# A diffusion layer on one core: the neighbourhood values' column blocks kept by row, and copied later

## The chip, the core and the metric

The kernel runs on one core of a Trainium2 chip. TensorE (PE) multiplies matrices, and its weight loads (PEld) run beside its products; VectorE (DVE), ScalarE (ACT) and GpSimd (POOL) work on elements; SyncE (SP) issues nearly all transfers, and 16 DMA engines carry them out. Each engine takes its own list of instructions in order and waits at semaphores for the others. The metric is the time of one execution in microseconds (us) on the device. All numbers are of one core.

## The reference, cut to what matters

One layer works on 1024 latent tokens (a grid of 16 rows by 64 columns) and 256 context tokens, 1024 wide. Half of the width goes through a gated DeltaNet (four heads of 128, scanned forward and backward in chunks), half through a neighbourhood attention (eight heads of 64). Then follow an output projection and a SwiGLU feed-forward.

```python
px = modulate(rms_norm(x, norm1_w[i]), sh1, sc1) @ w_in[i]
pc = modulate(rms_norm(ctx, norm1_w[i]), csh1, csc1) @ w_in[i]
...
dn_x, _, _ = gated_deltanet(px[..., :DN_IN], ..., s_ctx_f, s_ctx_b)
qx, kx, vx = na_qkv(px[..., DN_IN:], na_q_norm_w[i], na_k_norm_w[i])
qc, kc, vc = na_qkv(pc[..., DN_IN:], na_q_norm_w[i], na_k_norm_w[i])
na_x = neighborhood_attention(qx, kx, vx, kc, vc, na_rpb[i], rows)
x = x + g1 * (jnp.concatenate([dn_x, na_x], axis=-1) @ w_out[i])
x = x + g2 * swiglu(...)
```

In the neighbourhood attention a query sees 8 rows by 16 columns around it. The 64 columns are cut into four blocks of 16 queries, and all queries of a block read the same 32 columns of keys and values (`key_cols`); each query masks what lies outside of its window. The values that a column block needs are therefore 32 of each row's 64 columns, in all 16 rows: 512 tokens of 512 values.

## The kernel before, in words

The projections run from about 60 to 547 us, as a list of jobs. A job is one block of 128 output columns (or a wide one, whose result stays by token): `k`, `q`, `v` of the DeltaNet with their short convolutions, `nk`, `nq` of the attention, and `z`, the DeltaNet's output gate. The list ends with nq0 to nq2, q0, q1 (at the index `turn`), q2, q3, v0 to v3, nq3 and z0 to z3. For each job, in this order in the text:

- `prefetch` loads the weights of the job after it (L218, `wraw<-w_...` on SP). There is one raw buffer. ACT rounds it to a high part (L219, CAST `whi<-wraw`), POOL subtracts to get the low part (L221, `wlo<-wraw,whi`). There are two buffers of each part.
- PE makes the products in eight steps of 128 (L102, `blk<-hh,whi`, then `hl,whi`, then `hh,wlo`; hh and hl are the two parts of the tokens). `blk` with its number is the block's accumulator. A q, nq or z block takes 48 of these products (1024 tokens), a v block 72 (1280 tokens).
- After it ACT copies the block out (L506, `cr<-blk`; L483, `zt<-blk` for z). For q, k and v the five taps of the convolution follow on DVE (L515 and L520, `cacc<-cr,cw`), then an activation (L529, `cacc<-cacc`), and two jobs later the block's finish: its transposes on PE (L106, `m<-cst,cacc`) and what is stored from them.
- Beside the products, a step at a time, run background programs. `block_inverses` makes small inverses (N, L947 to L952). `preps` makes the twenty chunk systems of the DeltaNet: products `pr<-fx,kk` and `pr<-y,kk` on PE, with `kk` made on DVE (L1016) and copied on ACT (L1028), `y` copied on DVE (L1036), and stores `y_d` and `at_d` (L1052). `copies` issues the copies that this change is about.

The values of the attention, `nv_d`, are written by token in DRAM (L669). `vw_d` holds for each of the four column blocks (`cb`) its 32 columns of each row, by four groups of four rows (`ch`). The attention loads a column block of two heads at a time from it (L331, `vw<-vw_d`): 128 partitions by four groups of 128 values. Its loads of the first heads (L279 to L337: kT, qs, kh, kl, vc, bt, vw, v, y, kt) are issued at the end of the projections, once the chunk systems' buffers are free.

What is issued when isn't the order of the text: a scheduler sets each engine's list at build, by its own costs, within what the data allow. `tc.keep_in_program_order` holds the instructions that are given to it in the order in which they were written.

Of the kernel before, what the change touches and what calls it, by code (L numbers as in the profile page):

```python
# [9 lines left out]
F32 = mybir.dt.float32  # L10
# [18 lines left out]
BLKS = [0, 8, 24, 32]  # L29
# [62 lines left out]
def hybrid(ctx, tc, a, dbg):  # L92
    nc = tc.nc
    act, dve, pool, sp = nc.scalar, nc.vector, nc.gpsimd, nc.sync
# [16 lines left out]
    def pools(stack, name, side=None, bufs=1, **kw):  # L111
        if side:
            kw["side"] = side
        return stack.enter_context(tc.tile_pool(name=name, bufs=bufs, reuse_waits="tile", **kw))
# [6 lines left out]
    dram = ctx.enter_context(tc.tile_pool(name="dram", bufs=1, space=DRAM))  # L121
# [43 lines left out]
    nv_d = dram.tile([T, 512], F32, name="nv_d", tag="nv_d")  # L165
    nq_d = dram.tile([NAH, 2, ND, L], F16, name="nq_d", tag="nq_d")
    nk_d = dram.tile([2, NAH, ND, T], F16, name="nk_d", tag="nk_d")
    vw_d = dram.tile([128, 4, 4, 512], F32, name="vw_d", tag="vw_d")
    y_d = dram.tile([2, NCH, 128, 4, 128], F32, name="y_d", tag="y_d")
    at_d = dram.tile([2, 8, 128, 4, 128], F32, name="at_d", tag="at_d")  # L170
    x_d = dram.tile([128, 2, 2, NU, 32], F32, name="x_d", tag="x_d")
# [97 lines left out]
    def load(d, c, own=None):  # L269

        def tile(n):
            if own:
                return own.tile([128, 4, 128], F32, name=n, tag=f"{n}{d}")
            return (scan_v if n == "v" else scan_in).tile([128, 4, 128], F32, name=n, tag=n, bufs=3)

        old = chunks.pop(c, None)
        kT, qT, kt, v = old or (tile("kT"), tile("qT") if c >= 2 else None, tile("kt"), tile("v"))
        if not old:
            sp.dma_start(kT, kT_d[:, :, c * 128:(c + 1) * 128])  # L279
            sp.dma_start(fl(v), v_d[c * 128:(c + 1) * 128])  # L280
        y = tile("y")
        sp.dma_start(y, y_d[d, c])
        if not old:
            sp.dma_start(fl(kt), k_d[c * 128:(c + 1) * 128])
        at = None
        if c >= 2:
            if not old:
                sp.dma_start(qT, qT_d[:, :, (c - 2) * 128:(c - 1) * 128])
            at = tile("at")
            sp.dma_start(at, at_d[d, c - 2])  # L290
        if not old and c in TWICE:
            chunks[c] = kT, qT, kt, v
        ready[d, c] = kT, qT, kt, v, y, at, bool(old) or c not in TWICE
# [5 lines left out]
    def attention(nw):  # L299
# [18 lines left out]
        def biases(hp, half, cb):  # L318

            key = hp, half, CASE[cb]  # L320
            if tables[0] != key:
                out = lasting_bt[tables[1] % 2]
                for u, w0 in enumerate(WIN):
                    sp.dma_start(out[u][:, w0:w0 + 384], a["rpb"][2 * hp + u, half, CASE[cb]])
                tables[:] = key, tables[1] + 1
            return lasting_bt[(tables[1] - 1) % 2]

        def values(hp, half, cb):
            if (hp, cb) not in blocks:
                vw = nw.tile([128, 4, 128], F32, name="vw", tag="vw", bufs=3)  # L330
                sp.dma_start(vw, vw_d[:, cb, :, hp * 128:hp * 128 + 128])  # L331
                blocks[hp, cb] = vw
            return blocks[hp, cb][:, half:half + 3]

# [59 lines left out]
        heads = {0: [load(0), load(1)]}  # L394
        vcs = {0: context(0)}
        bt, vw = biases(*order[0]), values(*order[0])
        yield 1
        old = None
        for n, (hp, half, cb) in enumerate(order):
            at = n % len(TILES)  # L400
            if at in (4, 6) and hp + 1 < NAH // 2:
                heads.setdefault(hp + 1, []).append(load(2 * hp + at // 2))
                if at == 4:
                    vcs[hp + 1] = context(hp + 1)
            cur = pair(heads[hp], bt, vw, vcs[hp], half, cb, na[hp])
            next(cur)
            if old:
                next(old)
            if n + 1 < len(order):
                bt, vw = biases(*order[n + 1]), values(*order[n + 1])  # L410
            yield 1
            if old:
                next(old)
            old = cur
            yield 1
# [5 lines left out]
    with ExitStack() as bs:  # L421
# [3 lines left out]
        hp = pools(bs, "hp", "right")  # L425
# [653 lines left out]
        inv = len(jobs)  # L1079
        jobs += [Block("nk", i) for i in range(3)] + [Wide(0, zp), Block("nk", 3)]  # L1080
        jobs += [Block("nq", i) for i in range(3)] + [Block("q", 0)]
        turn = len(jobs)
        jobs += [Block("q", i) for i in (1, 2, 3)]
        later = len(jobs)
        values = inv + 3
        queries = range(turn - 1, later)
        jobs += [Block("v", i) for i in range(4)] + [Block("nq", 3)]
        gates = len(jobs)
# [2 lines left out]
        def windows():  # L1091
            vlat = nv_d[CT:].rearrange("(r c) d -> r c d", c=64)
            for cb in range(4):
                for ch in range(4):
                    sp.dma_start(vw_d[:, cb, ch], vlat[4 * ch:4 * ch + 4, BLKS[cb]:BLKS[cb] + 32])
                    yield

        copies = Background()

        def blk(n):  # L1100
            return jobs[n] if 0 <= n < len(jobs) and isinstance(jobs[n], Block) else None
# [9 lines left out]
        for n in range(2, len(jobs) + 2):  # L1111
            j = jobs[n] if n < len(jobs) else None
            if n == inv:
                bg2.drain()
                bg2s.close()
                early.close()
                psum.append(bs.enter_context(tc.tile_pool(name="psa", bufs=1, space=PSUM)))
                bg.add(block_inverses())
                bg.add(preps())
            if n == gates + 1:  # L1120
                bg.drain()
                late.close()
                cps.close()
                zo.append(pools(bs, "zo", "right", 2))
                fw = pools(attn, "nw", "left", 2)
                fill = attention(fw)
                next(fill)
                sl0 = pools(begins, "sl0", "left")
                KN, KB = (fw.tile([128, 2, NCH, 4], F32, name=n, tag=n, bufs=1) for n in ("KN", "KB"))
                dve.tensor_tensor(KN, KD, NB, OP.mult)  # L1130
                dve.tensor_tensor(KB, KD, B, OP.mult)
                for d in range(2):
                    load(d, ORDER[d][0], sl0)
            if n + 1 < len(jobs):
                jobs[n + 1].prefetch()
            fin = blk(n - 2) if n - 2 not in done else None
            fin = fin.finish() if fin else iter(())
            nrm = blk(n - 1)
            taps = nrm and nrm.later or iter(())
            if isinstance(j, Wide):  # L1140
                for t, _ in enumerate(j.tiles()):
                    next(fin, 0)
                    for _ in range(3):
                        next(taps, 0)
                    if t == 4 and nrm:
                        nrm.norm()
                        for _ in fin:
                            pass
                        fin = nrm.finish()
                        done.add(n - 1)  # L1150
                        nrm = None
                    bg2.step(2)
                    if n < turn:
                        bg.step(2)
                    if n >= turn:
                        bg.step(5)
            elif j:
                for k in range(KT):
                    j.mm([k])
                    next(taps, 0)  # L1160
                    next(taps, 0)
                    if k >= 3:
                        next(fin, 0)
                    bg.step(1 if n < turn else 3)
                    bg2.step(1)
                    copies.step(2)
                j.evac()
            for _ in fin:
                pass
            done.add(n - 2)  # L1170
            if isinstance(j, Wide) and n == values:
                copies.add(windows())
            if nrm:
                nrm.norm()
            if isinstance(j, Block) and j.later is None:
                j.silu()
# [213 lines left out]
    class Stream:  # L1390
# [67 lines left out]
        def next(self, n=2):  # L1458

            while len(self.got) < n:  # L1460
                self.make()
            out = [self.got.pop(0) for _ in range(n)]
            return out
# [400 lines left out]
```

## Time and profile before

| | |
|---|---|
| time, median of 3 runs | 1508.61 us (1508.04 to 1511.2) |
| the profiled execution | 1507.78 us |
| its span | 1506.0 us |
| mean granted clock of TensorE | 0.994 |
| DMA traffic | 267.35 MB, 178 GB/s over the span |
| the copies into `vw_d` | 16, issued from 220.3 to 260.6 us |
| the loads from `vw_d` | 16, issued from 531.1 to 726.0 us |

The profile is of one execution, and its times count from the span's start; 1.8 us of the execution lie outside of the span. Busy times are of each engine, and idle time matters on an engine only if others wait for it. In the lists of instructions, a row gives the start, the duration, the engine, the line and the operation with its output and inputs, and in brackets how long the engine sat idle before it and what ended that.

### The profile page before, as it was taken

The page shows a single profiled execution, that of the slowest core. Times are in us where ns is not written, and L with a number is a line of the kernel's source. Part 1 is how long each engine was busy: PE and PEld are TensorE (multiplying, and loading weights), DVE is VectorE, ACT ScalarE, POOL GpSimd, SP SyncE. Part 2 cuts the span into 40 slices and gives each one's busy share as a digit, 9 for nine tenths or more (in the row PEclk, how much of TensorE's full clock was granted, in tenths as well). Part 3 has the DMA queues.
Part 4 walks back from the last instruction along what each step waited for, and adds up shares of the span by engine and source line. Part 5 has one row for each costly group of instructions (what it writes and reads, how often), then busy time and mean ns, then how long its engine had stood idle before and what let it go on. Part 6 is the DMA issues. An engine that isn't in the chain of part 4 may idle for free.

```text
span 1506.0 us, 23093 instructions
## 1 busy us (share of the span) xinstructions
PE 1449.8 (96%) x8365; PEld 1201.0 (80%) x8365; DVE 1004.4 (67%) x1892; ACT 696.2 (46%) x1321; POOL 193.4 (13%) x223
## 2 busy tenths in 40 slices
PE   5999998899999999999989999999999999999998
PEld 2789787678877778887877878888888888888887
DVE  4886579455598427679966499666655557698642
ACT  6443461584266526566742374333333334354440
POOL 0154500343124221211100000000000000000000
PEclk9999999999999999999999999999999999999999
DMA  9377133555377799986349106333333334898742
GB/s 368 117 234 239 57 92 121 191 168 190 118 243 238 220 284 265 262 228 193 110 134 332 72 30 203 113 105 105 102 102 105 106 105 161 287 349 286 240 145 84
DMA packets 198851, 267.35 MB, mean 178 GB/s; under 512 B 15232, under 2 KB 106960, under 8 KB 197712
## 3 DMA queue, kind: packets, MB, share of 16 engines
q1 hardware_dynamic: 198016, 265.49, 54.7%
q8 instruction: 66, 1.08, 0.3%
q14 instruction: 49, 0.40, 0.1%
q10 hardware_dynamic: 720, 0.37, 0.1%
HBM read 201.01 MB, written 68.98 MB: 179 GB/s over the span
## 4 chain that ended last, share of the span: by engine, by line
PE 51%; DVE 6%; ACT 3%; DMA 2%; issue 1%; SPq 0%; ACTq 0%; DVEq 0%
PE ps L102 45%; PE sc L102 5%; PE sc L106 2%; DMA wad<-wa 1%; ACT pt L377 1%; ACT ex L365 1%; DVE ex L363 1%; DVE acc L255 1%; DVE x L1618 1%; DVE x L1594 0%; DVE ex L367 0%; DVE ulo L1449 0%; DVE lT L1589 0%; DVE ws L1444 0%; ACT x L1598 0%
## 5 line engine op out<-in xcount | busy, mean ns | idle before, releaser
L102 PE MATMUL ps<-hT,uhi 128*128 128x512 f32 x496 | 146.8, 390 | 0.8 <-DVE e L1739 0.7
L102 PE MATMUL ps<-lT,uhi 128*128 128x512 f32 x496 | 146.4, 389 | 0.0
L102 PE MATMUL ps<-hT,ulo 128*128 128x512 f32 x496 | 146.3, 389 | 0.0
L102 PE MATMUL blk<-hh,whi 128*128 128x512 f32 (+1 forms) x456 | 138.0, 393 | 2.4 <-ACT hh L748 1.7
L102 PE MATMUL blk<-hh,wlo 128*128 128x512 f32 (+1 forms) x456 | 129.7, 377 | 0.0
L102 PE MATMUL ps<-hB,uhi 128*128 128x512 f32 x436 | 129.1, 390 | 0.0
L102 PE MATMUL blk<-hl,whi 128*128 128x512 f32 (+1 forms) x456 | 129.0, 376 | 0.0
L102 PE MATMUL ps<-lB,uhi 128*128 128x512 f32 x436 | 128.8, 389 | 0.0
L102 PE MATMUL ps<-hB,ulo 128*128 128x512 f32 x436 | 128.8, 389 | 0.0
L1448 ACT CAST uhi<-ws 128x512 fp32r<-128x512 f32 x91 | 54.7, 622 | 145.5 <-PE ps L102 78.2
L1448 ACT CAST uhi<-wq 128x512 fp32r<-128x512 f32 x101 | 60.4, 621 | 132.8 <-PE ps L102 69.4
L1449 DVE TENSOR_TENSOR ulo<-wq,uhi 128x512 fp32r<-128x512 f32 x101 | 67.1, 687 | 65.6 <-ACT uhi L1448 36.4
L102 PEld LDWEIGHTS ps<-hT,uhi 128*128 128x128 f32 x496 | 93.0, 188 | 20.7 <-ACT uhi L1448 1.1
L102 PEld LDWEIGHTS ps<-lT,uhi 128*128 128x128 f32 x496 | 93.0, 188 | 19.7 <-DVE lT L1602 0.5
L102 PEld LDWEIGHTS ps<-hT,ulo 128*128 128x128 f32 x496 | 93.1, 188 | 19.4
L102 PEld LDWEIGHTS ps<-hB,uhi 128*128 128x128 f32 x436 | 81.8, 188 | 17.5 <-issue 0.5
L102 PEld LDWEIGHTS ps<-lB,uhi 128*128 128x128 f32 x436 | 81.8, 188 | 17.3 <-DVE lB L1602 0.4
L102 PEld LDWEIGHTS ps<-hB,ulo 128*128 128x128 f32 x436 | 81.8, 188 | 17.0
L102 PEld LDWEIGHTS blk<-hh,wlo 128*128 128x128 f32 x456 | 80.1, 189 | 17.6 <-issue 1.7
L102 PEld LDWEIGHTS blk<-hl,whi 128*128 128x128 f32 x456 | 80.7, 189 | 15.5
L102 PEld LDWEIGHTS blk<-hh,whi 128*128 128x128 f32 x456 | 76.5, 189 | 19.8 <-ACT hh L748 3.7
L1449 DVE TENSOR_TENSOR ulo<-ws,uhi 128x512 fp32r<-128x512 f32 x91 | 60.6, 685 | 36.2 <-ACT uhi L1448 28.0
(341 smaller groups left out, 3026.0 us busy)
## 6 DMA issues: line engine op xcount, KB each, us to landing
wq<-w_fo SPq DMA_DIRECT2D x99, 256.0 KB
wq<-w_gu SPq DMA_DIRECT2D x88, 256.0 KB
wad<-wa SPq DMA_DIRECT2D x64, 256.0 KB
t_d<-g SPq DMA_DIRECT2D x22, 512.0 KB
fr<-t_d SPq DMA_DIRECT2D x44, 256.0 KB
bt<-rpb SPq DMA_DIRECT2D x48, 192.0 KB
f_d<-g SPq DMA_DIRECT2D x33, 256.0 KB
fr<-f_d SPq DMA_DIRECT2D x33, 256.0 KB
```

The costliest lines, as they stand in the source:

```text
L102: i = nc.tensor.matmul(*args, **kw)
L106: i = nc.tensor.transpose(*args, **kw)
L255: dve.scalar_tensor_tensor(acc2, x, sc, acc2, op0=OP.mult, op1=OP.add)
L363: dve.tensor_tensor_reduce(ex, sc, bt, 1.0, -3.0e38, OP.add, OP.max, m[:, 0:1])
L365: act.activation(ex, ex, AF.Exp, bias=m[:, 1:2], accum_out=m[:, 2:3])
L377: act.copy(pt, sc)
L1448: act.copy(hi, self.raw[key])
L1449: dve.tensor_tensor(lo, self.raw[key], hi.bitcast(F32), OP.subtract)
L1618: dve.tensor_tensor(B[at][:, k], B[x][:, k], B.get(y, B["B11"])[:, k], OP.subtract)
```

## The change

`vw_d` becomes one array of 512 tokens for each column block, by row of the grid and then column. One copy for each column block takes the place of four: 16 rows in runs of 32 tokens by 512 values, 64 KB, where before a copy had four rows and 32 tokens, each token spread to another partition index, in runs of 2 KB. The bytes are the same, 4 MB. The sixteen copies went out two at a time from the job behind the second wide one on (from 220.3 us); the four go out one in each of the jobs q2, q3, v0 and v1, in the fifth of the eight steps, held in that order. The load `vw<-vw_d` keeps its shape, 128 partitions by four runs of 512 B.

```diff
-    vw_d = dram.tile([128, 4, 4, 512], F32, name="vw_d", tag="vw_d")
+    vw_d = dram.tile([4, 512, 512], F32, name="vw_d", tag="vw_d")
...
-                sp.dma_start(vw, vw_d[:, cb, :, hp * 128:hp * 128 + 128])
+                sp.dma_start(vw, vw_d[cb].rearrange("(n p) d -> p n d", p=128)[:, :, hp * 128:hp * 128 + 128])
...
-        values = inv + 3
...
             for cb in range(4):
-                for ch in range(4):
-                    sp.dma_start(vw_d[:, cb, ch], vlat[4 * ch:4 * ch + 4, BLKS[cb]:BLKS[cb] + 32])
-                    yield
+                tc.keep_in_program_order(nc.sync.dma_start(
+                    vw_d[cb].rearrange("(r c) d -> r (c d)", c=32),
+                    vlat[:, BLKS[cb]:BLKS[cb] + 32].rearrange("r c d -> r (c d)")))
+                yield
...
-                    copies.step(2)
+                    if k == 4:
+                        copies.step(1)
...
-            if isinstance(j, Wide) and n == values:
+            if n == turn:
                 copies.add(windows())
```

On PE the lists are the same up to the middle of q3; from there to the end of the projections many rows stand elsewhere, on all engines. Two places matter below.

The first is PE where v2 ends and v3 begins. Before, in PE's list (blk_3438 to 3440 are v2's accumulators, blk_3774 and 3775 v3's; pr_3800 is a product of a prep):

```order
L102 MATMUL blk_3438<-hh7_423,wlo_3311 128x256
L102 MATMUL blk_3439<-hh7_423,wlo_3311 128x512
L102 MATMUL blk_3440<-hh7_423,wlo_3311 128x512
L102 MATMUL blk_3774<-hh0_136,whi_3433 128x256
L102 MATMUL blk_3774<-hl0_137,whi_3433 128x256
L102 MATMUL blk_3774<-hh0_136,wlo_3434 128x256
L102 MATMUL pr_3800<-fx1_2479,kk_3522 128x96 x4
L102 MATMUL blk_3775<-hh0_136,whi_3433 128x512
```

The same place on PE in the changed kernel (blk_3426 to 3428 are v2's, blk_3762 to 3764 v3's; cacc_3415 is v1's convolution and cacc_3751 that of v2):

```order
L102 MATMUL blk_3426<-hh7_423,wlo_3298 128x256
L102 MATMUL blk_3427<-hh7_423,wlo_3298 128x512
L102 MATMUL blk_3428<-hh7_423,wlo_3298 128x512
L106 MATMUL m_3894<-cst_71,cacc_3415 128x128 x4
L106 MATMUL m_3929<-cst_71,cacc_3415 128x128 x4
L106 MATMUL m_3958<-cst_71,cacc_3415 128x128 x2
L106 MATMUL m_4176<-cst_71,cacc_3751 128x128 x4
L106 MATMUL m_4203<-cst_71,cacc_3751 128x128 x4
L102 MATMUL blk_3762<-hh0_136,whi_3421 128x256
L102 MATMUL blk_3763<-hh0_136,whi_3421 128x512
```

The transposes of v2 (cacc_3751) moved from the nq3 job, where they stand before, to the front of v3, right behind v2's own last products. On ACT the cast of v3's weights has moved too. Before, in ACT's list (whi_3433 are v3's weights, blk_3315 begins v1's copy-out):

```order
L529 ACTIVATE cacc_3303<-cacc_3303 128x1280
L612 COPY kk_3385<-m_3386 128x512
L612 COPY kk_3385<-m_3402 128x512
L219 CAST whi_3433<-wraw_3432 128x1024
L506 COPY cr_3428<-blk_3315 128x256
```

In the changed kernel ACT's list has it (whi_3421) behind v2's copy-out and activation (cr_3752, cacc_3751):

```order
L529 ACTIVATE cacc_3415<-cacc_3415 128x1280
L506 COPY cr_3752<-blk_3426 128x256
L506 COPY cr_3752<-blk_3427 128x512
L506 COPY cr_3752<-blk_3428 128x512
L529 ACTIVATE cacc_3751<-cacc_3751 128x1280
L219 CAST whi_3421<-wraw_3420 128x1024
```

It moved by a whole block and more: from ahead of v1's copy-out to behind v2's copy-out and activation.

The second place is SP at the last two weight loads, those of z2 and z3. Before, in SP's list (the y_d and at_d rows are the preps' last stores, zT_d and nq_d stores of z and nq3):

```order
L591 DMA v_d<-vt 128x10x128
L1052 DMA at_d<-at 128x512 x3
L218 DMA wraw<-w_z 128x8x128
L484 DMA zT_d<-zt 128x1024
L1052 DMA y_d<-y_2474 128x512
L1052 DMA y_d<-y_2475 128x512
L1052 DMA y_d<-y_2476 128x512
L574 DMA nq_d<-hl_4621 64x1024 x4
L1052 DMA y_d<-y_2477 128x512
L218 DMA wraw<-w_z 128x8x128
L279 DMA kT<-kT_d 128x4x128
L305 DMA qs<-nq_d 128x1024
```

In the changed kernel SP issues them here; ahead of the first row shown stand the last y_d store and thirteen more loads of the attention, from kT on, with no weight load among them:

```order
L337 DMA vc<-nv_d 128x2x128
L324 DMA bt_4711<-rpb 128x384 x2
L331 DMA vw<-vw_d 128x4x128
L284 DMA kt<-k_d 128x512
L279 DMA kT<-kT_d 128x4x128
L280 DMA v<-v_d 128x512
L282 DMA y<-y_d 128x512
L284 DMA kt<-k_d 128x512
L218 DMA wraw<-w_z 128x8x128
L484 DMA zT_d<-zt 128x1024
L324 DMA bt_4713<-rpb 128x384 x2
L331 DMA vw<-vw_d 128x4x128 x2
```

Both weight loads moved behind the attention's first 22 loads, the one of z2 by more than twenty rows. On PE the last product of the last prep (pr on y and kk) stands in both kernels ahead of z2; in the changed one it is the very last row ahead of it, and z2's and z3's 96 products follow in one piece.

## The prediction

> **What bounds the kernel now.** I read the totals and the slices first, to see which engine sets the time:
>
> ```profile
> PE 1449.8 (96%) x8365; PEld 1201.0 (80%) x8365; DVE 1004.4 (67%) x1892; ACT 696.2 (46%) x1321; POOL 193.4 (13%) x223
> PE   5999998899999999999989999999999999999998
> DMA  9377133555377799986349106333333334898742
> ```
>
> TensorE (PE) is busy for 96% of the span, and a slice below 9 is rare. So 55 us of the span are all that any change can win, while every microsecond in which PE is made to wait is lost in full. Next I read the windows of the projection phase, which holds all that the change touches (columns: window, its length, then busy time and count of PE, PEld, DVE, ACT and POOL, the granted clock, the DMA engines' share, GB/s):
>
> ```profile
> 240.00:260.00 20.00, 16.99 (x81) 13.61 (x79) 19.35 (x19) 3.58 (x5) 2.66 (x1) 0.99 0.29 112
> 260.00:280.00 20.00, 17.59 (x83) 14.36 (x84) 9.89 (x18) 6.46 (x9) 5.19 (x7) 0.84 0.38 130
> 280.00:300.00 20.00, 13.10 (x54) 9.96 (x54) 9.96 (x6) 14.61 (x24) 5.69 (x9) 0.93 0.68 225
> 500.00:520.00 20.00, 20.00 (x157) 14.31 (x157) 9.60 (x22) 14.20 (x23) 4.53 (x7) 1.00 0.62 198
> 520.00:540.00 20.00, 20.00 (x90) 16.58 (x89) 0.17 (x2) 3.11 (x5) 3.43 (x2) 1.00 1.02 289
> ```
>
> PE stands still for 12.3 us between 240 and 300, just behind the sixteen copies, and not at all from 500 to 540. In the two late windows, where the new order puts its work, there is nothing to win. Two waits make up the early 12.3 us (engine, line and operation that waited, what it waited for, us in total, times, longest):
>
> ```profile
> PE pr L102 <- DVE kk L1016: 6.9, 1, 6.9
> PE m L106 <- DVE N L952: 5.4, 1, 5.4
> ```
>
> The second is a chain of VectorE (DVE) products of the block inverses, on which no transfer has a say; it stays. The first hangs on the copies. On SyncE's (SP's) queue, in ScalarE's (ACT's) cast of the weights that the load behind them brings, and on PE:
>
> ```profile
> 237.17 9.99 SPq L1095 DMA_DIRECT2D vw_d<-nv_d  x6
> 247.26 2.36 SPq L669 DMA_DIRECT2D nv_d<-zt  x1
> 249.66 11.61 SPq L1095 DMA_DIRECT2D vw_d<-nv_d  x5
> 261.36 2.26 SPq L218 DMA_DIRECT2D wraw<-w_nqk  x1
> ```
>
> ```profile
> 270.81 0.62 PE L102 MATMUL blk<-hh,wlo 128*128 128x512 f32 x2
> 273.49 1.05 ACT L219 CAST whi<-wraw 128x1024 fp32r<-128x1024 f32 x1 [20.93 <-DMA wraw<-w_nqk]
> ```
>
> From 237.17 to 261.26 eleven copies and one store go through, 24.1 us; per copy that is 2.19 us for 256 KB, 119 GB/s, with the DMA share at 0.29 to 0.38. The weight load behind them lands so late that its cast starts at 273.49. A reader sees here what the old form costs: the queue, not the engines, is full.
>
> **The gain.** Sixteen copies go, and with them the block at 237 to 261. The weights would then be there long before; the cast must still wait for the buffer that PE's block up to 271.4 (270.81 and 0.62) reads, so it can start some 2.0 us sooner. What follows it on ACT and DVE leads to the kk product for which PE waits 6.9 us. I take 2.3 us, the 2.0 and a little less crowding on the way; the ends are 0 (the chain turns out to hang on something else) and 6.9 (the whole wait).
>
> **The four copies.** Each moves 1 MB in 16 runs. Their price is not in the trace. By the 119 GB/s of the old ones it is 8.8 us each; by the 289 GB/s of window 520 to 540 it is 3.6 us. They stand on SP behind the weight loads of q2, q3, v0 and v1 and ahead of those that are needed a block later (the shortest block lasts 10.9 us, by the copy-outs of z1 and z2 at 525.05 and 535.99 that are quoted below). At either price the next load still lands in time, so I take 0; below 0 nothing speaks for them, and the upper end is rival 3. For the rate, the Trainium skill ("DMA: Bandwidth & Descriptors", section on why a DMA increments its semaphore by 16) says that a transfer is shared over the largest number of engines up to 16 that divides the slowest dimension on both sides: 4 engines for the old 4 rows against 128, 16 for the new 16 against 16. The DMA share of 0.29 to 0.38 under a full queue agrees with 4 of 16 and some other traffic; by that rule a new copy runs at the full rate, and the sum stays as it is.
>
> **The new order.** The four copies may not be moved against each other, and the scheduler that writes the order at build comes out elsewhere from q3 on. The instructions are the same but for twelve copies fewer; every engine runs its list in order, so a row that stands too early makes all behind it wait. Nothing in the trace shows these places, and each is put together from durations of before.
>
> *v3's start on PE* (the first place shown with the change). The transposes of v2's convolution (cst,cacc) now stand ahead of v3's first product, and v3's cast stands behind v2's activation L529 on ACT. Both need all of v2's convolution, whose input is the block that PE has just ended. That chain, from a v block of before, on ACT, DVE and POOL:
>
> ```profile
> 390.51 1.05 ACT L219 CAST whi<-wraw 128x1024 fp32r<-128x1024 f32 x1 [2.38 <-PE blk L102]
> 391.47 1.34 ACT L506 COPY cr<-blk 128x256 f32<-128x256 f32 x3
> 401.75 1.27 ACT L529 ACTIVATE cacc<-cacc 128x1280 f32<-128x1280 f32 x1 [8.94 <-DVE cacc L520]
> ```
>
> ```profile
> 391.87 2.33 DVE L515 TENSOR_SCALAR cacc<-cr,cw 128x256 f32<-128x256 f32 x1 [9.44 <-ACT cr L506]
> 394.23 1.00 DVE L520 SCALAR_TENSOR_TENSOR cacc<-cr,cw,cacc 128x254 f32<-128x254 f32 x2
> 395.15 0.75 DVE L515 TENSOR_SCALAR cacc<-cr,cw 128x1024 f32<-128x1024 f32 x1
> 395.82 4.57 DVE L520 SCALAR_TENSOR_TENSOR cacc<-cr,cw,cacc 128x255 f32<-128x255 f32 x5
> 400.43 1.28 DVE L520 SCALAR_TENSOR_TENSOR cacc<-cr,cw,cacc 128x1022 f32<-128x1022 f32 x1
> ```
>
> ```profile
> 391.64 2.40 POOL L221 TENSOR_TENSOR wlo<-wraw,whi 128x1024 fp32r<-128x1024 f32 x1 [15.12 <-ACT whi L219]
> ```
>
> From the copy-out of the block at 391.47 to the end of the activation at 403.02 it takes 11.55 us, and then 1.05 for the cast: 12.6 us in which PE has nothing. The low part wlo (2.40 on POOL) is read by the third product of each step, and hides behind the six before it. In the old order the same 11.55 us ran beside a whole block of PE work: that cover is what goes. I take 12.6. The ends: 8, should the chain start earlier than PE's end, and 16, with wlo in full and the other DVE rows that stand between the taps.
>
> *z2's weights on SP* (the second place shown). Before, the load of z2's weights left SP a block ahead; now SP issues it behind the last y_d store and 22 loads of the attention. The rows of SP and ACT before:
>
> ```profile
> 503.24 0.55 SPq L218 DMA_DIRECT2D wraw<-w_z  x1
> ...
> 519.80 0.33 SPq L1052 DMA_DIRECT2D y_d<-y  x1
> 520.22 0.59 SPq L218 DMA_DIRECT2D wraw<-w_z  x1
> 520.90 0.68 SPq L279 DMA_DIRECT2D kT<-kT_d  x1
> ...
> 535.53 0.43 SPq L284 DMA_DIRECT2D kt<-k_d  x1
> ```
>
> ```profile
> 511.19 1.03 ACT L219 CAST whi<-wraw 128x1024 fp32r<-128x1024 f32 x1
> 525.05 1.09 ACT L483 ACTIVATE zt<-blk 128x512 f32<-128x512 f32 x2 [7.99 <-PE blk L102]
> 526.02 1.05 ACT L219 CAST whi<-wraw 128x1024 fp32r<-128x1024 f32 x1
> 535.99 1.09 ACT L483 ACTIVATE zt<-blk 128x512 f32<-128x512 f32 x2 [8.92 <-PE blk L102]
> ```
>
> z2's cast ran at 511.19, 14 us before z1 left PE (its copy-out is at 525.05). In the new order the y_d store needs the last pr product, and that is PE's last row ahead of z2. So from PE's end of z1: a copy of y and the store, 1.0 us (0.33 for the store, the rest is an estimate from the small DVE rows); the 22 loads (kT first, kt last), 520.90 to 535.96, 15.1 us; the issue of the weights, 0.6; their way, 3 us as an estimate, since the window 520 to 540 shows the engines full (1.02, 289 GB/s, so 512 KB alone take 1.8 us); the cast 1.05. Sum 20.7 us, and PE has nothing else, since z2 and z3 stand there without any other row between them. The ends: 15, if the loads go out without a pause, and 26, if the weights queue behind all of the 5.8 MB that such a window moves (20 us). z3's weights follow a block behind and stay covered.
>
> *The clock.* Each long stall is followed by slow products, as both waits of before show:
>
> ```profile
> 262.40:266.30 3.90, 3.89 (x18) 3.20 (x18) 1.72 (x5) 0.00 (x0) 0.00 (x0) 0.50 0.54 181
> 299.00:303.00 4.00, 3.91 (x16) 3.07 (x17) 0.72 (x2) 3.60 (x11) 2.53 (x8) 0.50 0.90 309
> ```
>
> About 4 us at half the clock cost 2.0 us a stall; two stalls, 4.0 us. The Trainium skill ("TensorE: Matmul & The Clock Gate", Part 1) gives the same window of about 3.4 us of activity before the clock is full again; by it the term would be 3.4 us for two.
>
> *Six smaller places.* At v0's start three preps (pr products that feed each other through ACT and DVE) stand bare on PE where before they lay between products of a block; at v1, v2, nq3 and z1 a cast stands behind the copy-out of the block just ended; in nq3 and z0 ten prep products lie back to back. One such round, on PE, ACT, PE:
>
> ```profile
> 504.70 1.03 PE L102 MATMUL pr<-fx,kk 128*128 128x96 f32 x8
> 505.77 0.48 ACT L1028 COPY kk<-pr 128x384 f32<-128x384 f32 x1 [0.32 <-PE pr L102]
> 506.55 0.99 PE L102 MATMUL pr<-y,kk 128*32 128x96 f32 x16
> ```
>
> From one pr to the next 1.85 us, of which PE works 1.03. At 0.8 of waiting a round, five to six rounds at v0 give 4.5; a cast behind a copy-out (1.34 and 1.05) gives up to 2.4 at v1, v2 and nq3, of which I take 1.6, 2.5 and 1.5; z0 gets 2, and z1, where tables and copies stand ahead of the cast too, 4. Sum 16 us, from 5 (most hidden by the slack of one block) to 24.
>
> *Attention's start.* Its loads come no later than before beside the end of z3, some sooner: -1.5 (0 to -3).
>
> **Sum**, against the profiled execution (1507.8; the median of the runs, 1508.6, is 0.8 above it): -2.3 + 0 + 12.6 + 20.7 + 4.0 + 16 - 1.5 = +49.5, so 1557.3, and 1558 against the median.
>
> **Rivals.**
> 1. *One large stall does not come.* If v3's 12.6 or z2's 20.7 with its 2 of clock is covered after all (say the store and loads go out while z1 still runs), and the small places cost 8 rather than 16: -2.3 + 12.6 + 2 + 8 - 1.5 = +19, 1527, or with z2's alone +27, 1536. For it: estimates of single stalls add up places that share slack. Against it: PE runs in order and at neither place is there a row to fill the gap. 0.14.
> 2. *Faster.* The window at 240 to 300 is the one place where PE waits for these copies. If the whole 6.9 us go, and all that the new order does to PE is to shift work between waits of the same length, the end is 1508.6 - 6.9 = 1502. It decides if v3's cast and z2's load both come before PE ends v2 and z1. Against it: both windows 500 to 540 are at 20.00 busy, so there is no wait to be given back, and z2's load stands behind a store that needs z1's last rows. 0.04; 0.02 for a change within 0.2%, about what a measurement of this kernel can tell from none.
> 3. *The copies are slow.* If a run of 64 KB were left to a quarter of the engines or less, 8.8 us each and more, the weights of v0 to v3 would come late as well: three times some 8 us on top, 1580. Against it: sixteen equal rows and a share of 1.02 where loads are well cut. 0.06.
>
> **Chances.** My forecast, both stalls and most of the small ones, 0.74; rival 1 0.14, rival 2 0.04 and 0.02 for no change, rival 3 0.06. The predicted time is the sum, 1558. The forecast's own bounds (v3 8 to 16, z2 15 to 26, the small places 5 to 24) do not all fall one way; half of the added distances gives 1541 to 1573. The range takes in rival 1 with z2's stall alone and ends short of rival 3: 1528 to 1576. Slower by over 0.2%: 0.74 + 0.14 + 0.06 = 0.94.
>
> **What would show it.** PE's waits in the new profile should name ACT's cast (or the transposes' cacc of L529) before v3 with 10 us or more, and ACT's cast L219 with some 20 us before z2, behind SP rows of kT, qs, kh, kl, bt and w_z in one piece; the clock should read 0.5 in the 4 us behind each. The wait of 6.9 us on kk should be 4 to 5, and the copies 2 to 9 us each on SP with no weight load late for them. It would be wrong if PE shows 20.00 in the window of z2's start, or if the new waits stand before other blocks than v3 and z2.

## The result and the profile after

The changed kernel takes 1570.68 us in the median (1566.7 to 1571.57, four runs), the kernel before 1509.13 on the same occasions: 1.0401 times as long, with a 95% interval from 1.038 to 1.0422. That is 61.6 us more, where 1558 was forecast. The profiled execution took 1566.7 us, its span is 1564.9.

The totals and slices of the changed kernel:

```profile
PE 1461.5 (93%) x8365; PEld 1210.1 (77%) x8365; DVE 997.7 (64%) x1892; ACT 697.9 (45%) x1321; POOL 193.3 (12%) x223
PE   5999998998978839999998999999999999999999
PEclk9999999999989969999999999999999999999999
```

PE does the same 8365 products, and its dips have moved: there is an 8 and a 7 where q3 to v3 lie, and two 8s and a 3 from nq3 to the z blocks, with 6 as the granted clock under the 3. PE's busy time is 11.7 us longer although it does no more work; 10.3 of them are counted below as lower clock. Its waits between 310 us (where nq2 is copied out) and 607 (the end of z3), of the changed kernel:

```profile
PE blk L102 <- ACT whi L219: 30.9, 4, 23.8
PE m L106 <- ACT cacc L529: 8.5, 1, 8.5
PE pr L102 <- DVE y L1036: 5.6, 6, 2.5
PE pr L102 <- DVE kk L1016: 5.4, 3, 2.3
```

With three more of 0.6 and 0.7 us they sum to 52.4 us. In the kernel before, the same stretch (to 547) has 1.5 us in all:

```profile
PE pr L102 <- DVE y L1036: 1.2, 2, 0.8
PE pr L102 <- ACT kk L1028: 0.3, 1, 0.3
```

The copy-out of nq2 came 2.7 us sooner than before (310.06 against 312.73), that of z3 59.8 later (606.70 against 546.86), and after it 0.9 are won back. So 62.5 us were lost between the two: 50.9 of waits, 10.3 of half clock (summed over windows of 2 us, busy time of PE by what was missing of the clock), and 1.3 that I can't place.

*The largest*, z2. The changed kernel on SP, then ACT and PE:

```profile
558.88 0.32 SPq L1052 DMA_DIRECT2D y_d<-y  x1
559.25 0.57 SPq L279 DMA_DIRECT2D kT<-kT_d  x1
...
574.41 0.43 SPq L284 DMA_DIRECT2D kt<-k_d  x1
574.88 0.58 SPq L218 DMA_DIRECT2D wraw<-w_z  x1
```

```profile
580.88 1.05 ACT L219 CAST whi<-wraw 128x1024 fp32r<-128x1024 f32 x1 [22.55 <-DMA wraw<-w_z]
```

```profile
581.97 1.22 PE L102 MATMUL blk<-hh,whi 128*128 128x512 f32 x2 [23.76 <-ACT whi L219]
```

PE ends its last pr product at 558.2. The store, the 22 loads in 15.6 us, 6.0 us from the issue of the weights to their cast, and the cast follow one another, with PE idle for 23.76 us. While the weights were on their way (574.88 to 580.88) the DMA engines' share was 1.09, at 380 GB/s: they shared the engines with the attention's loads.

*The second*, v3, on ACT and PE:

```profile
441.33 1.35 ACT L506 COPY cr<-blk 128x256 f32<-128x256 f32 x3 [5.43 <-PE blk L102]
450.85 1.27 ACT L529 ACTIVATE cacc<-cacc 128x1280 f32<-128x1280 f32 x1 [8.17 <-DVE cacc L520]
452.03 1.03 ACT L219 CAST whi<-wraw 128x1024 fp32r<-128x1024 f32 x1
```

```profile
452.18 1.97 PE L106 MATMUL m<-cst,cacc 128*128 128x128 f32 x8 [8.47 <-ACT cacc L529]
453.79 1.41 PE L102 MATMUL blk<-hh,whi 128*128 128x256 f32 x3
```

Between v2's last product and v3's first lie 12.1 us, 9.2 of them idle (8.47, and 0.69 ahead of a transpose of v1). The rest is transposes, which PE did elsewhere before.

*The clock*, in windows behind the waits at v3, z1 and z2 (length, busy times, clock, DMA share, GB/s):

```profile
452.00:457.20 5.20, 5.03 (x18) 4.44 (x19) 3.71 (x8) 1.06 (x2) 3.76 (x6) 0.50 0.00 0
535.00:540.00 5.00, 5.00 (x22) 4.12 (x22) 0.42 (x1) 4.86 (x12) 4.22 (x13) 0.57 0.16 58
582.00:586.50 4.50, 4.12 (x9) 2.82 (x10) 0.00 (x0) 0.00 (x0) 2.37 (x1) 0.50 0.56 158
```

A fourth stretch lies at 381 to 386, behind v0's waits, with a granted clock of 0.53. Each costs 2.4 to 2.7 us.

*The copies.* Each of the four takes SP 0.53 to 0.58 us, and the early load of weights now leaves SP as soon as its buffer is free:

```profile
252.87 0.60 SPq L218 DMA_DIRECT2D wraw<-w_nqk  x1
...
359.82 0.54 SPq L1093 DMA_DIRECT2D vw_d<-nv_d  x1
```

Its cast starts at 271.05 instead of 273.49, and PE's wait on kk is 3.26 us instead of 6.90. No weight load after q1 waits for a copy.

### The profile page after: what moved, and what is told of

Its sections match the earlier page's. It is cut to its first block, busy times and chain, and to the rows that moved or that the text cites. A ratio compares the mean times of both kernels' runs of the same rounds, so it can differ in the third digit from the quotient of the medians.

```text
span 1564.9 us, 23094 instructions
## 1 busy us (share of the span) xinstructions
PE 1461.5 (93%) x8365; PEld 1210.1 (77%) x8365; DVE 997.7 (64%) x1892; ACT 697.9 (45%) x1321; POOL 193.3 (12%) x223
## 4 chain that ended last, share of the span: by engine, by line
PE 49%; DVE 6%; ACT 3%; DMA 2%; issue 1%; SPq 0%; ACTq 0%; DVEq 0%
PE ps L102 43%; PE sc L102 4%; PE sc L106 2%; DMA wad<-wa 1%; ACT pt L377 1%; ACT ex L365 1%; DVE ex L363 1%; DVE acc L255 1%; DVE x L1619 1%; DVE x L1595 0%; DVE ulo L1450 0%; DVE lT L1590 0%; DVE ex L367 0%; DMA wraw<-w_out 0%; DMA at<-at_d 0%
## 5 line engine op out<-in xcount | busy, mean ns | idle before, releaser
L221 POOL TENSOR_TENSOR wlo<-wraw,whi 128x1024 fp32r<-128x1024 f32 x21 | 53.8, 2560 | 274.4 <-ACT whi L219 255.1
```

What stands on the lines that cost most here:

```text
L221: lo_engine.tensor_tensor(o, r, h.bitcast(F32), OP.subtract)
```

## The experiments

Two theories stood against each other: that the loss is all of the new order, and that the four large copies themselves, so late, hold something up. Ratios are to the kernel before, in the same rounds. In some of these kernels the lines of the text lie two lower than in the changed kernel.

**Loads and casts held ahead.** From q1 on, `issue_after` puts all that is written later on SP and ACT behind the weight load and its cast:

```diff
+            casts.append(act.copy(h, r))
...
             if n + 1 < len(jobs):
                 jobs[n + 1].prefetch()
+            with ExitStack() as first_:
+                if n >= turn and n + 1 < len(jobs):
+                    first_.enter_context(tc.issue_after(casts[-1].ins))
+                    first_.enter_context(tc.issue_after(casts_sp[-1].ins))
```

> The changed kernel with its four copies as they are, but from q1 on each weight load and each cast is held ahead of what is written after it on SP and on ACT; in the order that comes of it no cast stands behind the copy-out of the block before, and both z loads stand ahead of the attention's loads. Theory of the order: all the loss goes, 1503 to 1508 us, 2 to 5 below the kernel before, since the 2.7 us won at 260 to 300 stay. Rival, that the four copies (their rate, or the traffic at their time) hold up the weight loads: the copies still run in the blocks q2 to v1, so at least 20 of the 62 us stay, 1530 or more.

1533.89 us, ratio 1.0177 (1.0145 to 1.0208): 37 of the 62 us go and 24 stay. The theory's number was missed, and the time lies where the rival had it. This run alone doesn't settle why, since its order is neither that of before nor that of the changed kernel. Its waits between 300 and 572 are other ones:

```profile
PE blk L102 <- POOL wlo L223: 5.3, 2, 3.5
PE blk L102 <- ACT whi L221: 3.6, 3, 1.8
PE pr L102 <- DVE kk L1018: 3.1, 3, 1.3
PE blk L102 <- ACT cr L508: 2.3, 1, 2.3
```

No wait is over 3.5 us, and the stalls at v3 and z2 are gone. But holding some rows is a third order, in which preps and low parts come late in v3 to z1: with the smaller ones 15 us of waits and 8 us of half clock, and at the attention's start a wait of 2.9 us that was 1.0 before. With the early gain of some 2 us taken off, some 4 of the 25 us by which this profiled execution is longer than that of before stay unplaced.

**Sixteen copies, late.** The old copies, four in each of the jobs q2, q3, v0 and v1, held in place; PE, ACT, DVE and POOL have the lists of before, row for row.

```diff
-                    sp.dma_start(vw_d[:, cb, ch], ...)
+                    tc.keep_in_program_order(sp.dma_start(vw_d[:, cb, ch], ...))
...
-                    copies.step(2)
+                    if k == 4:
+                        copies.step(4)
...
-            if isinstance(j, Wide) and n == values:
+            if n == turn:
```

> The kernel before, its sixteen copies in runs of 2 KB unchanged in form, but issued four at a time in q2, q3, v0 and v1 and held there; the order of the other rows is that of before. Theory of the order: the queue is free at 237 to 261 as in the changed kernel and no row stands in the way later, so 1504 to 1509 us. Rival, that copies so late are what costs: four times 8.8 us of SP's queue (2.19 us each) hold up the weights of q3 to v2, 1515 to 1540.

1516.79 us, ratio 1.0042 (1.0026 to 1.0058). Here the rival is right, at the lower end of its range. On SP and ACT of this kernel:

```profile
358.46 7.18 SPq L1095 DMA_DIRECT2D vw_d<-nv_d  x3
365.74 0.64 SPq L218 DMA_DIRECT2D wraw<-w_conv  x1
```

```profile
376.51 1.04 ACT L219 CAST whi<-wraw 128x1024 fp32r<-128x1024 f32 x1 [3.58 <-DMA wraw<-w_conv]
```

The old form blocks the queue here as well, and in its new place it stands ahead of weights: v0's and v1's casts wait 3.85 and 3.58 us for them, ACT's copy-outs behind those casts come late, and PE waits 4.05 and 1.6 us at 368 to 378. Copies can cost there; those of the changed kernel, at 0.5 us of SP each, don't.

**Runs of 2 KB in the order of the change.** Both sides of each 1 MB copy are written with the 32 columns as a dimension of their own, which leaves the list of every engine as it was, row for row.

```diff
-                    vw_d[cb].rearrange("(r c) d -> r (c d)", c=32),
-                    vlat[:, BLKS[cb]:BLKS[cb] + 32].rearrange("r c d -> r (c d)")))
+                    vw_d[cb].rearrange("(r c) d -> r c d", c=32), vlat[:, BLKS[cb]:BLKS[cb] + 32]))
```

> The changed kernel with each of its four 1 MB copies written as 16 rows of 32 runs of 2 KB; every engine's order is that of the changed kernel. Theory of the order: nothing changes, 1565 to 1573 us, with PE waiting 23 to 24 us before z2 and about 9 before v3. Rival, that the runs of 64 KB are what makes the copies slow or fast: a difference of over 5 us, and copies that land in another time than the 2.8 to 9.0 us of the changed kernel.

1567.1 us in one run, with nearly the same waits, 24.57 before z2 and 8.47 before the transposes at v3. The landing times that the expectation names turned out to be those of the loads from `vw_d`; the trace gives none for the copies.

**The order of before, with the four late copies.** Beside the run above, only the description of the destination changes, to 512 rows of 2 KB; the diff is against the changed kernel:

```diff
-                    vw_d[cb].rearrange("(r c) d -> r (c d)", c=32),
-                    vlat[:, BLKS[cb]:BLKS[cb] + 32].rearrange("r c d -> r (c d)")))
+                    vw_d[cb], vlat[:, BLKS[cb]:BLKS[cb] + 32]))
```

With this the scheduler gives PE, ACT, DVE and POOL the lists of before, row for row, and SP too but for the copies themselves; the same bytes go out in the same four jobs. So its order hangs on how a transfer is described; why it comes out so isn't shown.

> The changed kernel with one thing written differently: the destination of each 1 MB copy is described as 512 rows of 2 KB instead of 16 of 64 KB, the source as 16 by 32 runs of 2 KB. The bytes, the four copies and the jobs in which they go out are the same; the lists of PE, ACT, DVE and POOL are row for row those of the kernel before. Theory of the order: the whole loss goes and the gain at 260 to 300 stays, 1504 to 1508 us, no wait over 2 us on PE between 300 and 547. Rival, that late copies hold up SP and the weights as the sixteen late ones did (8 us): 1512 to 1520, with casts that wait for w_conv.

1507.26 us, ratio 0.9979 (0.9962 to 0.9995): all of the loss is gone, and 3.0 us are won. Its waits on PE between 300 and 543 are those of before:

```profile
PE pr L102 <- DVE y L1036: 1.2, 2, 0.8
PE ps L102 <- ACT zt L483: 1.0, 1, 1.0
PE pr L102 <- issue: 0.3, 1, 0.3
PE pr L102 <- ACT kk L1028: 0.2, 1, 0.2
```

and the early wait is short, as in the changed kernel:

```profile
295.85 1.13 PE L102 MATMUL pr<-fx,kk 128*128 128x96 f32 x8 [3.27 <-DVE kk L1016]
```

With the run before it this settles the main question: in one order runs of 2 KB and of 64 KB take 1567 and 1567 to 1572 us, and in the other the same copies at the same jobs take 1507. It is the order. This version is also 0.2% faster than the kernel before.

**Runs of 8 KB in the order of before.** `vw_d[cb]` as 128 rows of four tokens.

```diff
+                    vw_d[cb].rearrange("(p n) d -> p (n d)", n=4),
+                    vlat[:, BLKS[cb]:BLKS[cb] + 32].rearrange("r (q c) d -> r q (c d)", c=4)))
```

> As the run before it, but with the destination as 128 rows of 8 KB and the source as 16 by 8 runs of 8 KB; the order is again that of before. Theory of the order: the same time as with runs of 2 KB, within 2 us. Rival, that longer runs matter: 3 us or more faster, and copies that land sooner.

1507.21 us, ratio 0.9978 (0.9962 to 0.9993), the same as with 2 KB.

**Four copies early.** The changed kernel's copies at the old time, two a step after the second wide job:

```diff
-                    if k == 4:
-                        copies.step(1)
+                    copies.step(2)
...
-            if n == turn:
+            if isinstance(j, Wide) and n == inv + 3:
```

> The changed kernel's four copies at the time of the old sixteen, right after the second wide job; from q1 on the order is that of before. Theory of the order: no stall at v3 or z2, and the queue is free by 237, so 1503 to 1510 us (up to 4 more if the one prep product that stands bare ahead of q0 makes PE wait). Rival, that four copies of 1 MB crowd the engines whenever they run: the weight load of the nq blocks comes late by 4 times 3.6 us and more, 1515 or above.

1532.45 us, ratio 1.0152 (1.012 to 1.0184), missed. The stalls at v3 and z2 aren't there, but a new one is, on PE and, for its cause, on DVE:

```profile
313.04 1.17 PE L102 MATMUL pr<-fx,kk 128*128 128x96 f32 x4 [22.10 <-DVE kk L1016]
```

```profile
297.02 1.28 DVE L556 SCALAR_TENSOR_TENSOR cacc<-cacc,qkw,cr 128x1024 f32<-128x1024 f32 x1 [3.75 <-ACT cr L551]
298.22 2.49 DVE L569 TENSOR_TENSOR hl<-cacc,hl 128x512 f16<-128x512 f32 x4
300.62 1.51 DVE L967 STREAM_TRANSPOSE ut<-WK 128x1280 f32<-128x1280 f32 x1
302.17 1.49 DVE L970 TENSOR_TENSOR WK<-WK,NB 128x1280 f32<-128x1280 f32 x1
```

The second half of the inverses' results (L967, L970) now stands on DVE behind the norms of two nq blocks; in the kernel before it ran at 283.50 and 286.32. The preps' inputs and with them kk come that much later. It is once more a matter of rows that stand too early (the norms), at a place that I had not looked at when I wrote the expectation.

**Four copies early, order kept.** The 512-row form without `keep_in_program_order`. The scheduler then puts all four at 242.9 us, and PE's list is that of before.

> The four copies with 512 rows of 2 KB, not held in order: the scheduler puts all four right after the values are stored, ahead of the last nq loads; PE's list is that of before. Theory of the order: the 22 us that the four early copies cost before came from the rows that moved with them, so here 1503 to 1509. Rival, that four copies early crowd the engines: 1515 or more, with the wait on kk L1016 well above 7 us again.

1508.15 us, ratio 0.9985 (0.9972 to 0.9998). So four early copies don't crowd anything either; the 22.1 us above were the order.

**Two halves.** The holding of the first experiment, from z1's weights on alone (`n >= gates`), and only for those of the blocks before z0 (`turn <= n < gates - 1`):

> The changed kernel with the weight loads and casts of z1 to z3 held ahead of what is written after them on SP and ACT; up to z0 the order is that of the changed kernel, so the waits ahead of v0 to v3 stay. If the wait of 23.8 us before z2 is a price of its own: it goes, with the 3.7 before z1 and 4 to 5 us of half clock, 1533 to 1541 us. Rival, that the work merely waits elsewhere, since the attention's loads now come later and the preps are still crowded into the z blocks: 1548 to 1560.

1542.49 us, ratio 1.021 (1.0187 to 1.0233): 28.2 us less than the changed kernel. It is 1.5 above the upper end named, and no wait stands before z2 any more. A little of it comes back at the attention's start, whose loads now go later:

```profile
580.29 3.78 PE L102 MATMUL ps<-v,y 128*128 128x128 f32 x16 [4.19 <-ACT zt L485]
```

> The changed kernel with the weight loads and casts of v0 to nq3 held ahead of what is written after them; those of z0 to z3 are left, so z2's load stands behind the attention's 22 loads as in the changed kernel. If the waits before v0 to v3 (17 us) and the half clock behind two of them (5 us) are prices of their own: they go, 1546 to 1553 us. Rival, that the preps which filled those places then crowd the z blocks, as they seemed to where all loads were held ahead (24 us stayed there): the 28 us of z2's repair on top of that kernel's 1534, 1557 to 1566.

1549.51 us, ratio 1.0247 (1.0214 to 1.0281): 21.2 us less, inside the first range. z2's wait is there as before (22.74). Each repair is worth about its own stall when it is made alone. Both together give 36.8, not 49.4: most of the first experiment's 24 us are waits of preps and low parts of up to 3.5 us and the half clock around them, which come with its own order.

**A control.** The holding in the kernel before:

> A control: the kernel before, with its own sixteen copies, and its weight loads and casts held ahead as in the first run of this study. If the holding itself costs the 24 us that stayed in that run: 1525 or more. If they came from the changed order of the preps: 1507 to 1514.

1509.64 us, ratio 1.0004 (0.9989 to 1.0019). Holding loads and casts ahead costs nothing by itself. PE's list is not that of before here either (it differs from some 345 us on), so another order need not cost anything; it depends on the rows.

**Copies of four rows.** Sixteen copies of four rows, in runs of 64 KB, late.

```diff
+                for ch in range(4):
+                    tc.keep_in_program_order(nc.sync.dma_start(
+                        vw_d[cb, 128 * ch:128 * ch + 128].rearrange("(r c) d -> r (c d)", c=32),
+                        vlat[4 * ch:4 * ch + 4, BLKS[cb]:BLKS[cb] + 32].rearrange("r c d -> r (c d)")))
```

> The changed kernel with sixteen copies of four rows, in runs of 64 KB, late and held in order. If the number of rows in a copy sets how many engines carry it: 256 KB on 4 engines land no sooner than 1 MB on 16, about 4.5 to 5.5 us, and SP is held up by the copies of a group. Rival, that long runs are what is fast: 256 KB land in 3 us or less. The order is one with late casts like the changed kernel's, so the time is 1560 to 1590.

1572.19 us in one run. The landing times asked for aren't in the trace. From the windows of 1 us: a group of four, issued from 359.92 to 362.32, shows traffic until about 371, some 11 us for 1 MB; the changed kernel's copy, issued at 359.82 in like traffic, is through by 365.0. Such short windows are rough, with shares up to 1.84. SP isn't held up as it was at that place by runs of 2 KB (2.40 us for four, where three took 7.18), so that part of the expectation was missed.

## Why the prediction was right, and where its terms were off

The direction, the two places and their mechanism came out as forecast; 1570.7 lies in the range, 12.7 above the point. Between the profiled executions the change is 58.9 us against a sum of 49.5, so 9.4 us are what the terms have to answer for. That the time lies in the range is in part luck: half of the distances of the three bounds named is 10.7 down and 8.4 up, so 1547 to 1566 and not the 1541 to 1573 of the prediction, and 1570.7 lies above that. The stated range held because it was drawn wider, out to its rivals.

The terms, forecast against measured:

- *The gain*: -2.3 against -2.7, by the chain named (cast at 271.05, kk wait 3.26).
- *The copies*: 0 against 0. Why the old form would not have been free in the new place, the second experiment shows.
- *v3*: 12.6 against 9.2 of idle time. The chain of copy-out, taps, activation and cast took 11.7 us (441.33 to 453.06), 0.9 less than forecast; I counted all of it as idle, though 2.2 us of transposes lie in it, and the end of the block before overlaps its start by 0.4.
- *z2*: 20.7 against 23.8, and 0.4 for the low part. The 22 loads took 15.6 us for 15.1. What was under-sized is the way of the weights, 6.0 us where I put 3: the engines were full with the attention's loads (share 1.09), as the upper end of that term had it. This miss and that of v3 all but cancel, which is luck.
- *The clock*: 4.0 against 10.3, the largest miss. I gave half clock to the two long stalls alone. Four places had it, v0 and z1 too, where waits of 0.2 to 3.7 us lie close together, and each cost somewhat more than 2.0.
- *The six small places*: 16 against 19.0, place by place 4.5 for v0 (4.5 measured), 1.6 and 2.5 for v1 and v2 (1.5 and 2.0), 1.5 for nq3's cast (none), 2 for z0 with the preps in nq3 ahead of it (4.9), 4 for z1 (6.0).
- *Attention's start*: -1.5 against -0.9.

Off these come the 1.5 us of waits that the kernel before has in the same stretch, and 1.3 us stay unplaced; with both the measured terms make up the 58.9.

Of the signs that were named, the wait of some 20 us before z2, the rows of SP ahead of it and the clock of 0.5 came. The wait before v3 was 8.5 us and not 10 or more, the wait on kk 3.3 and not 4 to 5, and a copy takes SP 0.5 us and not 2 to 9. Three readings were slightly off without changing the sum: PE's idle time before is 56.2 us, not 55; the eleven old copies alone take SP 21.6 us, 1.96 each, since the 24.1 hold a store too; and 2.5 was taken for v2 where up to 2.4 was said.

Rival 1, that one large stall does not come, fell: both came. Rival 2 took the early wait as the only one that matters; it is what remains when the order is kept, with 3.0 us rather than 6.9. Rival 3, slow copies, is wrong for these four and right for the sixteen old ones at that place, with some 8 us: in that kernel's profile q1's cast comes 2.6 us sooner than before, z3's 5.8 later.

## What to carry to other kernels

When a scheduler sets the order, a transfer that is moved or described otherwise can move hundreds of rows on engines that have nothing to do with it; here that cost 62 us, for a transfer whose own change is worth 3. Compare the lists of both kernels, and look for rows whose inputs come from the block just ended (a cast, a transpose, a weight load behind a row of others); price each by the chain in the old trace, and add half clock for each cluster of waits, not only for the long ones. If the order is what costs, keep the transfer and change what the scheduler sees of it: here another description of the destination turned a loss of 62 us into a gain of 3.

## What the runs showed of the hardware

For copies of 16 source rows, the length of the runs within DRAM made no difference to the kernel's time that these runs can tell: 2 KB and 8 KB gave 1507.26 and 1507.21 us, 2 KB and 64 KB in the other order 1567.1 and 1566.7 to 1571.6. The number of rows did make a difference to how fast a copy passes. In the kernel with sixteen late copies the engines' share while little but such copies ran is

```profile
392.00:394.00 2.00, 2.00 (x15) 1.84 (x14) 0.00 (x0) 0.59 (x1) 0.00 (x0) 1.00 0.27 108
397.00:401.00 4.00, 4.00 (x21) 3.22 (x20) 3.27 (x4) 1.61 (x4) 2.40 (x1) 1.00 0.30 102
```

0.27 to 0.30 and 102 to 108 GB/s with four rows a copy, and 1 MB in sixteen rows passes in about 5 us beside other loads. By the rule of the Trainium skill that the prediction used ("DMA: Bandwidth & Descriptors", section on why a DMA increments its semaphore by 16) four rows give 4 of 16 engines, a share of 0.25 as an estimate, and the 0.27 to 0.30 agree with it. Whether the length of the runs matters to SP with four rows isn't settled: three copies in runs of 2 KB held it up for 7.18 us at 358 us, four in runs of 64 KB for 2.40 at 360, but the first four in runs of 2 KB, at 343, took only 2.9.

The clock was less regular than I had assumed. The same wait of 3.3 us on kk was followed by half clock in the changed kernel (299 to 303) and by none where the order was kept:

```profile
299.00:303.00 4.00, 4.00 (x19) 3.44 (x19) 1.96 (x4) 2.14 (x8) 3.02 (x8) 0.50 0.65 140
```

```profile
299.00:303.00 4.00, 4.00 (x33) 3.10 (x32) 2.43 (x5) 3.41 (x12) 3.55 (x9) 1.00 0.71 164
```

In the changed kernel the clock was half at v0 too (0.53 from 381 to 386), where no wait is over 2.52 us. The Trainium skill ("TensorE: Matmul & The Clock Gate", Part 1) has the clock fall after an idle window of about 3.4 us, a window that runs freely and doesn't start with the work. None of these waits is that long, so that length alone doesn't explain the half clock behind them; that the window runs freely may be why one wait of 3.3 us was followed by it and another not. No run here varies that alone.
